# Passage from the projections to the branch products: four rows loaded over the freed activation, splits given out ahead, last merge gates in two buffers

## Chip, cores and metric

The kernel runs on one core of a Trainium2 chip. The metric is the time of one execution on the device, in microseconds (us). The profiler records one execution; the span is the time from its first instruction to its last.

## What is computed

Two layers over a sequence of 1024 rows with 1024 columns each. The change lies in the first one, `hybrid_layer`. Cut to what matters:

```python
u = layer_norm(x) * (1 + scale) + shift          # shift, scale, gate from silu(c) @ w_ada
proj = u @ w_in + b_in                           # ten projections, the last 3 x 1024 wide
y_a = pool branch of a_v * pool_scale * silu(a_g)
y_b = b_b * causal_dwconv(b_c * b_h) * silu(b_g)
y_c = silu(layer_norm(h_c)) * silu(c_g)          # h_c: causal_dwconv of 31 taps
g_m = sigmoid(merge)                             # three gates
m = g_m[0] * (y_a @ w_branch[0]) + g_m[1] * (y_b @ w_branch[1]) + g_m[2] * (y_c @ w_branch[2])
out = m @ w_out
return layer_norm(ALPHA * x + gate * out, ln_g, ln_b)
```

The second layer (attention, spatial gating and a gated MLP) follows and isn't touched.

## The kernel before

**Precision.** A float32 matrix product is made of three products of rounded parts: every operand is split into a high part (a cast on ACT) and a low part (a subtraction on DVE), `hilo` at L164. One product of 1024 by 1024 by 128 columns of weights, a slot, is 48 matmuls of 128 x 128 by 128 x 512: two halves of the columns, eight blocks k, three part products.

**Projections.** The transposed activation u lies on the chip as high part A0 and low part A1. Most projections run in pairs by a scheme with seven products of half size in place of eight (`run_two`, L395), whose operands are quarters of u and sums of quarters, held in B0 (high) and B1 (low). The order of the seven is 1, 6, 5, 2, 7, 3, 4; 1, 2 and 4 read quarters of u, the others read sums. The weights of a pair are split into parts a, b, c, d; five tiles on the right side of the memory hold them (`pair_tiles`, L1848), in this order from the start: a high, a low, c high, b low, c low; the high part of b lies elsewhere. In the trace, `A,w` and `B,w` are such products.

**Epilogues.** The results of a pair leave in `epi_store` (L832): one ACT operation (a sigmoid for the merge gates) into the tile e, and a store to DRAM from SP's queue. In the last part of the projections `n_e` is 1, so e is a single buffer: the second result waits until the store of the first has landed.

**The passage.** The last projections are those of a_v for group 0 and the last pair of merge gates (`add_merge`, i = 22). Then `pool_slot(0)` (L957) makes the pool products of that group: its `pre` empties the background queue, flushes the epilogue of the last pair, opens the pool ws for plain weights over the tiles of the pairs (two raw buffers wr from the start on, then two wh, then two wl, 1024 words each), starts the loads of the first branch weights (`dma_ahead`, L242), splits rows 0 to 3 of y_b, and splits the first weights (`split_ahead`, L251). Rows 0 to 3 of y_b have been loaded into raw and sums of the pool cw by `end` (L1020), during the last pair. `split_y` (L1035) writes the parts to new tiles over B0 and B1.

The results of the pool products, two rows of ya, leave through two buffers s (tag s, two of them, handed out in turn; the doubling sums of the pool use the same two before, an even number of times) and are stored from POOL's queue (L990).

`open_q` (L1048) closes the pools cw and ca and opens cq in their place. cw holds raw and sums, 2048 words each. ca begins behind it with pw (512 words), v (1040), and two s (1040 each); cn, ph, pl and others follow. cq is laid out in the order of first use: three g, one cb, four ld (tiles of 1024 words), mu_h, rs_h. So g and cb cover raw and sums. The second ld row that is handed out lies in the fourth place and covers part of the second s. A load into a new tile waits until the tiles below it are free. `open_q` loads the first gate g, rows 4 to 7 of y_b into ld, two more gates, splits the four rows, loads the statistics mu_h and rs_h and then c, and applies Silu to c on ACT.

**Branch products.** Slots d = 0 to 7 for branch 1 (y_b), then 0 (y_a), then 2 (y_c). For branch 1 and d = 0 the order is by k, so that the first half of the slot reads only rows 0 to 3. In `pre` a slot of branch 1 below d = 4 loads two rows of w_ada (`gate_dot`, L1095, into the ld tiles) and puts their dot products with silu(c) (DVE) in the background; the slot's result is multiplied by its gate on DVE behind them. Between d = 1 and d = 2 stands `stat_h` (products that sum mu_h and rs_h over the partitions, then moments, a reduction and a reciprocal root), between d = 2 and d = 3 `spread_h` (products `cst,wide` that spread its result).

Each engine and each DMA queue works in its own program order; waits are by semaphores between them.

Of the kernel before, what the change touches and what calls it, by code (L numbers as in the profile page):

```python
# [11 lines left out]
F = mybir.dt.float32  # L12
# [10 lines left out]
P = 128  # L23
# [83 lines left out]
class Kernel:  # L107
# [603 lines left out]
    def block1(self):  # L711
        nc, I = self.nc, self.I
        c0x, cwx = ExitStack(), ExitStack()
        T = {}
        d = lambda n, m=NK: [self.dram.tile([P, 1024], F, name="%s%d" % (n, i)) for i in range(m)]
        h_sp, ya_sp, yb_sp, ag_sp, cg_sp, mg_sp, m_sp = (
            d("h_sp"), d("ya_sp"), d("yb_sp"), d("ag_sp"), d("cg_sp"), d("mg_sp", 24), d("m_sp"))
# [33 lines left out]
        def e_tile():  # L751
            return self.c1.tile([P, 1024], F, tag="e", name="e", bufs=self.n_e)
# [78 lines left out]

        def epi_store(ct, func, sp, i):  # L832
            def one(ps, k):
                e = e_tile()
                self.act(e, ps, func, bias=self.bias_in(ct + k))
                nc.sync.dma_start(sp[i + k], e)
            return lambda x, y: [Task(0, lambda: one(x, 0)),
                                 Task(0, lambda: one(y, 1), 4 if self.n_e == 1 else 0)]

# [2 lines left out]
        def epi0():  # L842
# [13 lines left out]
                               name="start"))  # L856
# [39 lines left out]
        for what in "M G C5 B5 M M C6 G M B6 M C7 G M B7 M G M M".split():  # L896
# [4 lines left out]
            elif what[0] == "C":  # L901
                j = int(what[1])
# [54 lines left out]
        def pool_slot(g):  # L957
            s = {}

            def pre():  # L960
                while self.bgq:
                    self.bgq.popleft()()
                pairs.flush()
                if g == 0:
                    self.open_right("ws")
                    self.resume()
                    self.dma_ahead()
                    for j in range(4):
                        split_y(1, j)
                    self.split_ahead(1)  # L970

            def mm():
                wh, wl = T["pwr"]
                s["ps"] = [self.pair(), self.pair()]
                for c in range(2):
                    for h in range(2):
                        hs = slice(h * H, (h + 1) * H)
                        for k in range(2):
                            ph, pl = T["pool", 2 * g + k]
                            ks = slice((k * 2 + c) * P, (k * 2 + c + 1) * P)  # L980
                            self.mm3(s["ps"][c][:, hs], (wh[:, ks], wl[:, ks]), (ph[:, hs], pl[:, hs]),
                                     k == 0, k == 1)

            def one(c):
                if g:
                    e = e_tile()
                else:
                    e = self.c1.tile([P, 1040], F, tag="s", name="s", bufs=2)[:, 0:1024]
                self.act(e, s["ps"][c], AF.Identity, scale=self.par("pool_scale", 2 * g + c))
                (nc.sync if g else nc.gpsimd).dma_start(ya_sp[2 * g + c], e)  # L990

            def epi():
                pairs.todo = [Task(0, lambda c=c: one(c)) for c in range(2)]
                if g == 0:
                    pairs.flush()

            self.slots.append(Slot([], mm, epi, pre=pre, name="pool%d" % g))

        def open_a():
# [10 lines left out]
        for g, rest in ((3, "AA"), (2, "AM"), (1, "AM"), (0, "M")):  # L1010
            pair_u(A_V + 2 * g, A_V + 2 * g + 1, epi_av(g))
            for what in rest:
                if what == "M":
                    add_merge()
                else:
                    i = next(pool_gate)
# [14 lines left out]
        def open_y(n):  # L1031
            a, b = ("A0", "A1") if n == 0 else ("B0", "B1")
            T["Y", n] = (self.big(a, R), self.big(b, R))

        def split_y(n, j):  # L1035
            if ("Y", n) not in T:
                open_y(n)
            self.hilo(T["Y", n][0][:, j], T["Y", n][1][:, j], T["ld"].pop((n, j)))

        def load_y(n, j):  # L1040
            if j < 8 and (n, j) not in T["ld"]:
                t = T["ld"][n, j] = self.c1.tile([P, 1024], F, tag="ld", name="ld", bufs=4)
                nc.sync.dma_start(t, {0: ya_sp, 1: yb_sp, 2: h_sp}[n][j])
                if n != 1:
                    t = T["ld"]["g", n, j] = self.c1.tile([P, 1024], F, tag="ld", name="ld", bufs=4)
                    nc.sync.dma_start(t, (cg_sp if n else ag_sp)[j])

        def open_q():  # L1048
            self.ca.close()
            cwx.close()  # L1050
            self.ca = ExitStack()
            self.c1 = self.ca.enter_context(self.pool("cq", reuse_waits="tile"))
            T["g"], T["mi"] = {}, {}
            load_g(1, 0)
            T["g"][1, 1] = self.c1.tile([P, 1024], F, tag="g", name="g", bufs=3)
            T["g"][1, 2] = self.c1.tile([P, 1024], F, tag="g", name="g", bufs=3)
            T["cb"] = self.c1.tile([P, 1024], F, name="cb2")
            for j in range(4, 8):
                load_y(1, j)
            for j in (1, 2):  # L1060
                nc.sync.dma_start(T["g"][1, j], mg_sp[8 + j])
            for j in range(4, 8):
                split_y(1, j)
            self.mu_h = self.c1.tile([P, 1024], F, name="mu_h")
            self.rs_h = self.c1.tile([P, 1024], F, name="rs_h")
            nc.sync.dma_start(self.mu_h, st_sp[0])
            nc.sync.dma_start(self.rs_h, st_sp[1])
            nc.sync.dma_start(T["cb"], I["c"])
            self.act(T["cb"], T["cb"], AF.Silu)

        def load_g(n, d):
            if d < 8 and (n, d) not in T["g"]:
                T["g"][n, d] = self.c1.tile([P, 1024], F, tag="g", name="g", bufs=3)
                nc.sync.dma_start(T["g"][n, d], mg_sp[n * 8 + d])
                if n != 1:
                    T["mi"][n, d] = self.c1.tile([P, 1024], F, tag="mi", name="mi", bufs=2)
                    nc.sync.dma_start(T["mi"][n, d], m_sp[d])
# [33 lines left out]
        def branch(n, d, bg):  # L1111
# [37 lines left out]
            def epi():  # L1149
# [12 lines left out]
                else:  # L1162
# [3 lines left out]
                                   name="br%d.%d" % (n, d)))  # L1166

        self.slots.append(Slot(pre=open_q))
        held = len(self.slots)
        for n in (1, 0, 2):  # L1170
# [1058 lines left out]
```

## Time and profile before

| | us |
|---|---|
| three timed runs, median | 2711.1 |
| lowest and highest | 2710.7 and 2712.61 |
| the profiled execution | 2704.81 |
| its span | 2703.0 |

Microseconds in the rows count from the span's start. Engines: PE makes matrix products, PEld loads its weights, DVE and ACT work elementwise, POOL likewise, SP issues DMAs. "SPq" and "POOLq" are the DMA issues of these engines. L143 is the matrix product's helper line, L159 DVE's two-operand helper, L165 the cast in `hilo`, L156 the activation's helper, L247 the weight load, L1043 the load of a row into ld, L990 the store of ya. `B<-raw` and `B<-ld` are splits of y_b, `e<-pp` the merge gates, `s<-pp` the ya rows, `wh<-wr` and `wl<-wr` the parts of the weights. Brackets give the idle time of the engine just before and what ended it.

### The profile page before, as it was taken

The page shows a single profiled execution, that of the slowest core. Times are in us where ns is not written, and L with a number is a line of the kernel's source. Part 1 is how long each engine was busy: PE and PEld are TensorE (multiplying, and loading weights), DVE is VectorE, ACT ScalarE, POOL GpSimd, SP SyncE. Part 2 cuts the span into 40 slices and gives each one's busy share as a digit, 9 for nine tenths or more (in the row PEclk, how much of TensorE's full clock was granted, in tenths as well). Part 3 has the DMA queues.
Part 4 walks back from the last instruction along what each step waited for, and adds up shares of the span by engine and source line. Part 5 has one row for each costly group of instructions (what it writes and reads, how often), then busy time and mean ns, then how long its engine had stood idle before and what let it go on. Part 6 is the DMA issues. An engine that isn't in the chain of part 4 may idle for free.

```text
span 2703.0 us, 29526 instructions
## 1 busy us (share of the span) xinstructions
PE 2622.2 (97%) x11688; PEld 2143.6 (79%) x11688; DVE 1881.6 (70%) x2141; ACT 981.1 (36%) x1284; POOL 182.4 (7%) x178
## 2 busy tenths in 40 slices
PE   5999999999999997999999999999999999999998
PEld 3888887888788776877887788888888888887776
DVE  7789988899886664566564254546647788885576
ACT  5322233333343333222243255542323334343333
POOL 4000000000000000000032100000000000000220
PEclk9999999999999998999999999999999999999999
DMA  6111121222232225676342121112532222216964
GB/s 234 55 63 63 63 86 70 102 86 94 86 129 109 99 108 186 255 287 253 125 156 83 68 86 65 68 32 100 180 130 78 86 79 85 88 61 234 276 147 149
DMA packets 102380, 324.63 MB, mean 120 GB/s; under 512 B 11489, under 2 KB 12001, under 8 KB 102242
## 3 DMA queue, kind: packets, MB, share of 16 engines
q1 hardware_dynamic: 95474, 309.65, 31.9%
q0 software_dynamic: 6768, 13.11, 2.6%
q8 instruction: 91, 1.49, 0.2%
q14 instruction: 47, 0.39, 0.0%
HBM read 247.21 MB, written 75.50 MB: 119 GB/s over the span
## 4 chain that ended last, share of the span: by engine, by line
PE 75%; DVE 10%; DMA 7%; ACT 4%; issue 3%; SPq 1%; POOL 1%; DVEq 0%; ACTq 0%; POOLq 0%
PE pp L143 73%; DMA A<-g_sp 1%; DVE h L162 1%; DMA B<-x_sp 1%; DVE sums L159 1%; DVE ld L159 1%; DVE wl L159 1%; DVE A L159 1%; PE pm L143 1%; DVE g L159 1%; DVE B L159 1%; ACT e L156 1%; PE pp L146 1%; PE pm L146 1%; DMA mg_sp<-e 1%
## 5 line engine op out<-in xcount | busy, mean ns | idle before, releaser
L143 PE MATMUL pp<-A,wh 128*128 128x512 f32 x2432 | 769.7, 392 | 13.5 <-DVE A L159 9.0
L143 PEld LDWEIGHTS pp<-A,wh 128*128 128x128 f32 x2432 | 454.4, 188 | 115.1 <-DVE A L159 10.9
L143 PE MATMUL pp<-A,wl 128*128 128x512 f32 x1296 | 506.0, 390 | 2.8 <-DVE wl L159 2.8
L143 PE MATMUL pp<-B,A 128*128 128x512 f32 x1676 | 487.8, 390 | 1.2 <-DVE B L159 1.1
L143 PE MATMUL pp<-A,w 128*128 128x512 f32 x1664 | 443.4, 392 | 12.8 <-DVE pp L159 6.7
L143 PEld LDWEIGHTS pp<-A,w 128*128 128x128 f32 x1664 | 313.7, 189 | 83.3 <-DVE pp L159 10.3
L143 PE MATMUL pp<-B,w 128*128 128x512 f32 x1136 | 374.7, 389 | 0.0
L143 PEld LDWEIGHTS pp<-B,A 128*128 128x128 f32 x1676 | 313.9, 188 | 68.1 <-DVE B L159 2.3
L162 DVE SCALAR_TENSOR_TENSOR h<-p,par_t,h 128x1024 f32<-128x1024 f32 x240 | 312.8, 1303 | 4.7
L143 PEld LDWEIGHTS pp<-A,wl 128*128 128x128 f32 x1296 | 243.8, 188 | 55.4 <-DVE wl L159 4.5
L143 PE MATMUL pp<-B,wh 128*128 128x512 f32 x800 | 263.8, 395 | 15.6 <-ACT B L165 8.3
L159 DVE TENSOR_TENSOR wl<-wr,wh 128x1024 fp32r<-128x1024 f32 (+1 forms) x120 | 144.3, 1203 | 172.7 <-ACT wh L165 168.8
L143 PEld LDWEIGHTS pp<-B,w 128*128 128x128 f32 x1136 | 213.2, 188 | 44.3
L143 PEld LDWEIGHTS pp<-B,wh 128*128 128x128 f32 x800 | 151.3, 190 | 49.3 <-ACT B L165 9.2
L165 ACT CAST wh<-wr 128x1024 fp32r<-128x1024 f32 (+1 forms) x120 | 118.5, 989 | 188.3 <-PE pp L143 159.2
L162 DVE SCALAR_TENSOR_TENSOR z<-pp,par_t,z 128x1023 f32<-128x1023 f32 x88 | 112.6, 1280 | 48.0 <-ACT z L156 47.0
L143 PE MATMUL pp<-yh,xh 128*128 128x512 f32 x308 | 122.6, 398 | 5.9 <-ACT yh L165 5.9
L373 ACT CAST w<-raw 128x1024 fp32r<-128x1024 f32 x50 | 52.6, 1053 | 207.8 <-PE pp L143 141.0
L143 PE MATMUL pp<-yl,xh 128*128 128x512 f32 x308 | 123.1, 400 | 4.4 <-DVE yl L159 4.4
L143 PE MATMUL pp<-A,A 128*128 128x512 f32 x324 | 126.7, 391 | 0.1
L143 PE MATMUL pp<-B,wl 128*128 128x512 f32 x320 | 125.9, 393 | 0.0
L143 PE MATMUL pp<-yh,xl 128*128 128x512 f32 x308 | 121.1, 393 | 0.0
(278 smaller groups left out, 3187.4 us busy)
## 6 DMA issues: line engine op xcount, KB each, us to landing
raw<-in_w_in SPq DMA_DIRECT2D x66, 512.0 KB, 4.1
wr<-in_w_in SPq DMA_DIRECT2D x63, 512.0 KB, 3.5
raw<-in_w_up SPq DMA_DIRECT2D x34, 512.0 KB, 5.2
mg_sp<-e SPq DMA_DIRECT2D x24, 512.0 KB, 4.1
wr<-in_w_br SPq DMA_DIRECT2D x24, 512.0 KB, 5.9
g<-mg_sp SPq DMA_DIRECT2D x24, 512.0 KB, 5.4
A<-g_sp SPq DMA_DIRECT2D x44, 256.0 KB, 6.3
g_sp<-z SPq DMA_DIRECT2D x21, 512.0 KB, 3.0
```

The lines of the kernel that those rows point to most:

```text
L143: return self.nc.tensor.matmul(*a, **k)
L146: self.nc.tensor.transpose(*a)
L156: return self.nc.scalar.activation(out, in_, func, **kw)
L159: return self.nc.vector.tensor_tensor(out, a, b, op)
L162: self.nc.vector.scalar_tensor_tensor(out, a, s, b, op0, op1)
L165: self.nc.scalar.copy(hi, src)
L373: self.nc.scalar.copy(t.__dict__[which][0], src)
```

## The change

In `epi_store`, the last merge pair puts its second result into a buffer s, not into e, and both its results are stored from POOL's queue instead of SP's. In `pool_slot(0)`, the splits of rows 0 to 3 stand ahead of the flush of that pair's epilogue, not behind the start of the weight loads. Behind the weight loads, a new tile is opened over A0, and rows 4 to 7 of y_b are loaded into it from SP's queue. In `open_q` the loads of these four rows into ld are gone; their splits stay where they were and read the new tile.

```diff
@@ -831,9 +831,13 @@
 
         def epi_store(ct, func, sp, i):
             def one(ps, k):
-                e = e_tile()
+                last = sp is mg_sp and i == 22
+                if last and k:
+                    e = self.c1.tile([P, 1040], F, tag="s", name="s", bufs=2)[:, 0:1024]
+                else:
+                    e = e_tile()
                 self.act(e, ps, func, bias=self.bias_in(ct + k))
-                nc.sync.dma_start(sp[i + k], e)
+                (nc.gpsimd if last else nc.sync).dma_start(sp[i + k], e)
             return lambda x, y: [Task(0, lambda: one(x, 0)),
                                  Task(0, lambda: one(y, 1), 4 if self.n_e == 1 else 0)]
 
@@ -960,13 +964,18 @@
             def pre():
                 while self.bgq:
                     self.bgq.popleft()()
+                if g == 0:
+                    for j in range(4):
+                        split_y(1, j)
                 pairs.flush()
                 if g == 0:
                     self.open_right("ws")
                     self.resume()
                     self.dma_ahead()
-                    for j in range(4):
-                        split_y(1, j)
+                    t = self.big("A0", F)
+                    for j in range(4, 8):
+                        T["ld"][1, j] = t[:, j]
+                        nc.sync.dma_start(t[:, j], yb_sp[j])
                     self.split_ahead(1)
 
             def mm():
@@ -1055,8 +1064,6 @@
             T["g"][1, 1] = self.c1.tile([P, 1024], F, tag="g", name="g", bufs=3)
             T["g"][1, 2] = self.c1.tile([P, 1024], F, tag="g", name="g", bufs=3)
             T["cb"] = self.c1.tile([P, 1024], F, name="cb2")
-            for j in range(4, 8):
-                load_y(1, j)
             for j in (1, 2):
                 nc.sync.dma_start(T["g"][1, j], mg_sp[8 + j])
             for j in range(4, 8):
```

## Rows read from the trace of the kernel before

**Rows 1.** The page, section 1: busy us, share of the span, instructions.

```profile
PE 2622.2 (97%) x11688; PEld 2143.6 (79%) x11688; DVE 1881.6 (70%) x2141; ACT 981.1 (36%) x1284; POOL 182.4 (7%) x178
```

**Rows 2.** PE's timeline: start us, us, operation, out and in, count [idle before, releaser].

```profile
1035.42 2.88 PE L143 MATMUL pp<-B,A 128*128 128x512 f32 x12
...
1039.04 3.02 PE L143 MATMUL pp<-A,w 128*128 128x512 f32 x12 [0.74 <-DVE pp L159]
...
1047.15 0.39 PE L143 MATMUL pp<-ph,pwr 128*128 128x512 f32 x1
...
1053.62 1.22 PE L143 MATMUL pp<-B,wh 128*128 128x512 f32 x2 [6.08 <-ACT wh L165]
...
1068.67 0.79 PE L143 MATMUL pp<-B,wh 128*128 128x512 f32 x1 [7.42 <-ACT B L165]
...
1087.97 0.40 PE L143 MATMUL pp<-B,wl 128*128 128x512 f32 x1
...
1102.71 2.02 PE L143 MATMUL pp<-cst,wide 128*128 128x128 f32 x16
```

**Rows 3.** Windows: length, busy PE/PEld/DVE/ACT/POOL, granted PE clock, DMA share, GB/s.

```profile
1050.00:1055.00 5.00, 1.34 (x3) 0.62 (x3) 4.72 (x6) 3.80 (x5) 0.00 (x0) 0.54 0.59 217
```

**Rows 4.** ACT's timeline, columns as PE's.

```profile
1042.83 1.12 ACT L156 ACTIVATE e<-pp,par_t 128x1024 f32<-128x1024 f32 x1 [5.79 <-DVE pp L159]
...
1046.70 1.12 ACT L156 ACTIVATE e<-pp,par_t 128x1024 f32<-128x1024 f32 x1 [2.75 <-DMA mg_sp<-e]
...
1047.71 1.98 ACT L165 CAST B<-raw 128x1024 fp32r<-128x1024 f32 x2
...
1052.52 1.04 ACT L165 CAST wh<-wr 128x1024 fp32r<-128x1024 f32 x1 [0.94 <-DMA wr<-in_w_br]
...
1054.78 2.11 ACT L156 ACTIVATE s<-pp,par_t 128x1024 f32<-128x1024 f32 x2
...
1067.57 1.04 ACT L165 CAST B<-ld 128x1024 fp32r<-128x1024 f32 x1 [10.68 <-DMA ld<-yb_sp]
...
1079.91 1.28 ACT L156 ACT_TABLE_LOAD   x1 [5.42 <-DMA cb<-in_c]
```

**Rows 5.** Timeline of the DMA issues of SP's queue and of POOL.

```profile
1048.25 8.24 SPq L247 DMA_DIRECT2D wr<-in_w_br  x4
...
1056.22 0.80 POOL L990 DMA_DIRECT2D ya_sp<-s  x1 [25.47 <-ACT s L156]
...
1057.06 10.79 SPq L1043 DMA_DIRECT2D ld<-yb_sp  x4
...
1057.21 0.55 POOL L990 DMA_DIRECT2D ya_sp<-s  x1 [0.19 <-issue]
...
1070.12 0.83 SPq L1068 DMA_DIRECT2D cb<-in_c  x1
```

**Rows 6.** Waits of SP's queue, 1040 to 1120: us in total, times, longest.

```profile
SPq L1043 <- DMA ya_sp<-s: 9.1, 1, 9.1
```

**Rows 7.** DVE's timeline, columns as PE's.

```profile
1042.10 0.70 DVE L159 TENSOR_TENSOR pp<-pp,two 128x512 f32<-128x512 f32 x1 [2.31 <-PE pp L143]
...
1048.78 2.36 DVE L159 TENSOR_TENSOR B<-raw,B 128x1024 fp32r<-128x1024 f32 x2 [5.98 <-ACT B L165]
...
1053.60 2.54 DVE L159 TENSOR_TENSOR wl<-wr,wh 128x1024 fp32r<-128x1024 f32 x2 [0.19 <-ACT wh L165]
```

**Rows 8.** Tile wr, 1040 to 1115: its loads, from issue to landing.

```profile
DMA to landing us min/median/max: 3.4/4.2/7.5
```

**Rows 9.** Tile s, 1040 to 1115: its two stores, from issue to landing.

```profile
DMA to landing us min/median/max: 7.8/8.6/9.3
```

**Rows 10.** DMA issues of the whole run: count, KB each, median us to landing.

```profile
t<-in_w_dn POOLq DMA_DIRECT2D x11, 256.0 KB, 5.0
```

**Rows 11.** Timeline of POOL and DVE in the down-projection.

```profile
2488.05 1.90 POOL L1976 DMA_DIRECT2D B<-in_w_dn  x2 [13.03 <-ACT yh L165]
...
2489.24 0.69 DVE L159 TENSOR_TENSOR yl<-yr,yh 128x512 fp32r<-128x512 f32 x1
```

## Prediction

> **What bounds the kernel now.** I read the page first. PE is busy 97% of the span [rows 1], so a change of order can win only where PE stands still, or where it runs at its lower clock. I then read PE's timeline around the edited lines. The largest two holes lie in the passage that the diff touches: 6.08 us before the first branch product, and 7.42 us before the second half of that same product [rows 2]. The windows add that in 1050 to 1055 the granted clock is 0.54 of 2.4 GHz, which is the 1.2 GHz level for nearly the whole window [rows 3]. So the passage costs more than its holes.
>
> What ends each hole is told by the timelines of the other engines.
> - First hole. PE is done with the pool products at 1047.4 (last one 1047.15, next possible 0.23 later) [rows 2]. ACT passes the second merge gate only at 1046.70, held by the store of the first from the single buffer e [rows 4]. SP issues the branch weights behind the second gate's store, at 1048.25 [rows 5]. The weights land, ACT casts them at 1052.52, and PE starts at 1053.62.
> - Second hole. Rows 4 to 7 of y_b are loaded from 1057.06 on, and the second of these loads waits 9.1 us for a store of ya [rows 5, 6]; ACT casts row 4 at 1067.57 [rows 4].
> - Behind it stands the load of c, issued at 1070.12 after all of these and landed when ACT goes on at 1079.91 [rows 4, 5]. Silu(c), the adaLN dots and the statistics of h follow on ACT and DVE, up to the spread products, which start at 1102.71 [rows 2].
>
> **Scales.** Twelve products take 2.88 us with an end of 0.39 [rows 2], so one per (2.88 - 0.39) / 11 = 0.227 us, and one branch product (48) 10.9 us. The second branch product ends at 1087.97 + 0.23 = 1088.2, so the first ended at 1077.3. From 1088.2 to the spread at 1102.71 PE does the statistics and the third product: 14.5 us. From the landing of c to the spread it is 1102.71 - 1079.91 = 22.8 us, on ACT, DVE and SP; I take this stretch over as it is, since in it each step is issued by the one before.
>
> **Splits given out ahead.** Four high casts on ACT (1.98 per two [rows 4]) now stand before the merge gates. They write over the sums in B0/B1, last read by the product of 1035.42, which ends at 1038.3 [rows 2]. ACT is idle there until the gate at 1042.83 [rows 4], so the casts run 1038.3 to 1042.3 and cost nothing; without that cover they would cost 4.0. Their low parts stand on DVE behind the combination at 1042.10 [rows 7]: from 1042.8, four at 1.18 end at 1047.5, and the first weight's low part (1.2 [rows 7]) at 1048.7.
>
> **Merge gates.** The second gate takes a buffer s and no longer waits 2.75 us for a store [rows 4]: gates at 1042.83 and 1043.95, ending at 1045.0. The two stores go from SP to POOL, so SP has nothing before the weights. The first weight buffer lies over the pair's a, read last by the fourth of its seven products; the second over its c, free when the final product ends at 1042.0 (1039.04 + 3.02 [rows 2]). So SP issues the weights at 1042.1 at the latest, landing takes 4.2 (3.4 to 7.5 [rows 8]), and ACT casts them right behind the gates, 1045.0 to 1047.1. PE can start at 1047.4 and waits for the low part from 1047.9 to 1048.7: about 0.9 where it was 6.08. Its first 24 products then end at 1053.7, at full clock, since PE kept its clock after the hole of 0.74 at 1039.04, while both holes of over 6 us were followed by slow products [rows 2].
>
> **Rows 4 to 7 over A0.** The activation is read last by the product that ends at 1042.0; the four loads follow the weights on SP, 0.4 each, so 1042.5 to 1044. No later load is held, for SP had nothing else to do before. DMA is idle there. Row 4 lands near 1046.5, the last by 1054 (estimated, if the POOL stores take half of the engines from 1046 on). These loads wait no more for ya.
>
> **What the change adds.** Buffers s are two. The second gate now takes the one that is next, so the first ya row takes the other and the second ya row must wait until the gate's store has landed from POOL. Queued behind that ya row on ACT are the high casts of rows 4 to 7, and PE waits for those. POOL stores of 512 KB landed 7.8 and 9.3 after issue, some 0.3 after their ACT operation [rows 4, 5, 9]; the nearest lower row is 5.0 for 256 KB [rows 10]. I take 9.3, the second of a pair beside SP loads, which is the like case: issue 1045.3, landed 1054.6, ya 1.1 to 1055.7, high cast of row 4 1.05 to 1056.7, low cast to 1057.95, the remaining 23 products 5.2. The first branch product ends at 1063.2 against 1077.3: **PE's own gain 14.1**.
>
> The second added wait is on SP. The new pool's tiles start over raw and sums (4096 words: three g and c). With the ld rows gone from their place, mu_h and rs_h now come next: rs_h covers words 1024 to 2048 of the closed pool, and there, behind pw (512) and v (1040), begins the first s (at 1552). So the load of rs_h waits for the second ya store, and c and the adaLN rows stand behind it on SP. That is the 9.1 us wait of before [rows 6], moved. Ya issue 1056.0, landing 7.8 (the first of a pair in [rows 9]), 1063.8; rs_h issue 1063.9, c 1064.3, landing 4.6 (a load with one ahead, between 4.2 and the 7.5 of [rows 8]): 1068.9. The spread comes 22.8 later, 1091.7. PE is there at 1063.2 + 10.9 + 14.5 = 1088.6 and waits some 3. So c sets the end: **1102.7 - 1091.7 = 11.0 us**. Behind the spread the order and the bytes are those of before, so I carry the shift to the end.
>
> **Sum.** The profiled execution took 2704.81 (span 2703.0), the median is 2711.1, 6.3 more, spread over the whole run; the gain is taken off the median: 2711.1 - 11.0 = 2700.1. Bounds: with both POOL stores at 5.0, the second ends at 1050.3, the split is in time, the first product ends near 1059.2, PE reaches the spread at 1084.6 and c allows the same: gain 18.1, 2693.0. With 9.3 for both and 9.7 for c (issue 1070.12 to 1079.91 [rows 4, 5]): c at 1075.5, gain 4.4, 2706.7.
>
> **Rivals.**
> 1. *Quick stores* (5 to 6 us each): PE is the bound, 14.5 to 18.1 gained, about 2694. For it: DMA is idle before 1042. Against it: 7.8 and 9.3 [rows 9], the only POOL stores of this stretch. The Trainium skill ("DMA: Bandwidth & Descriptors", section on the anatomy of one DMA, SWDGE path) gives about 2.0 us plus bytes over 436 GB/s, an estimate of 3.2 for 512 KB; by it this rival would be the outcome, and the trace disagrees with 7.8 and 9.3 beside other traffic.
> 2. *POOL's issue is held while DVE works.* Then the gates' stores go out when DVE's low casts end, 1042.8 + 4.7 + 2.4 = 1049.9; landed 1059.5, ya store 1068.7, c 1073.8, gain 6.1: 2705.0. The Trainium skill ("SBUF — State Buffer", "SBUF: two separate sides") says that a DVE operation in a two-port mode keeps GpSimd from writing descriptors. Against it: POOL issued two loads in 1.90 us while DVE made such low casts, about its usual pace [rows 11].
> 3. *Late c*: the bound of 9.7 above, or a gain given back in later stages: 0 to 5 us, about 2707.
> 4. *Slower.* Two POOL stores in series now stand before c. With a for each, c lands at 1045.3 + a + 1.4 + a + 0.5 + 4.6 = 1051.8 + 2a. That meets 1079.9 of before at a = 14.1, and from there the change loses; at a = 18, because SP's 3 MB of weights, y rows and gates are served first, it loses 7.9: 2719.0. Against it: 9.3 is the largest landing of such a store [rows 9].
> 5. That A0 comes free later than I read: with the loads issued at 1047.4, after the pool products, row 4 would land near 1052, still ahead of ACT's turn at 1055.7. It changes nothing and goes with the forecast.
>
> **How the numbers follow.** Forecast 0.60, rival 1 0.17, rival 2 0.07, rival 3 0.10, rival 4 0.06. About 0.2% (5.4 us) is what a measurement of this kernel can tell from no change. Rival 2 lies at that edge, half to each side: faster 0.81, same 0.13, slower 0.06. The range 2692.5 to 2706.5 takes in the forecast, rivals 1 and 2 and the bounds, and leaves out most of 3 and all of 4.
>
> **What would show it.** PE's hole before the first branch product under 1.5; the hole before its second half 1 to 4, ended by ACT's cast of row 4, which follows the second ya row on ACT, which waits for the DMA of the gate's store. SP waiting at the load of rs_h for the ya store. ACT's Silu of c at 1066 to 1072, and a hole of some 3 us on PE before the spread. I am wrong if rs_h doesn't wait, if Silu stands after 1075, or if holes of several us appear behind the spread.

## The result, and the profile after

The changed kernel takes 2697.5 us (median of four runs, 2691.2 to 2700.5) against 2711.3: ratio 0.9945, 95% interval 0.9927 to 0.9963. That is faster by more than the 0.2% that can be told from no change, at 2.6 us under the forecast of 2700.1.

To compare traces, count from the start of the last pool product; it is the last product that PE makes alike in both programs. Two lengths serve for every kernel below. The **passage** goes from there to the start of the spread products. **Mark 4** is where DVE begins to multiply the fourth branch product's result by its gate; it takes in what a late spread or a low clock costs behind the passage. Before, the passage is 1102.71 - 1047.15 = 55.56 [rows 2], and mark 4 stands at 1115.67 - 1047.15 = 68.52. After, they are 1091.01 - 1045.22 = 45.79 and 1103.98 - 1045.22 = 58.76, both 9.8 less. Mark 4 in DVE's timeline, before and after:

```profile
1115.67 1.23 DVE L159 TENSOR_TENSOR g<-pp,g 128x1024 f32<-128x1024 f32 x1 [0.60 <-PE pp L143]
```

```profile
1103.98 1.22 DVE L159 TENSOR_TENSOR g<-pp,g 128x1024 f32<-128x1024 f32 x1 [0.67 <-PE pp L143]
```

The profiled spans differ by 2703.0 - 2689.4 = 13.6. Of that 1.9 lies ahead of the last pool product (1047.15 - 1045.22), 9.8 in the passage, and 1.9 behind it. The 1.9 ahead is there before the first instruction that stands elsewhere (the load of the first branch weight, issued at 1030.93 after): DVE makes a sum of the pool (`s<-v`) at 1031.83 before and at 1029.87 after. The passage is what the change did; the rest is taken up with the first experiment.

The page of the changed kernel, first its span, then section 1 (busy us, share of the span, instructions):

```profile
span 2689.4 us, 29519 instructions
...
PE 2616.5 (97%) x11688; PEld 2140.1 (80%) x11688; DVE 1880.0 (70%) x2141; ACT 980.4 (36%) x1284; POOL 183.2 (7%) x180
```

PE does the same 11688 products and shows the same 97% [rows 1]: the page can't tell where 10 us went. PE's timeline of the changed kernel can; it answers to [rows 2]:

```profile
1045.22 0.39 PE L143 MATMUL pp<-ph,pwr 128*128 128x512 f32 x1
...
1046.58 0.50 PE L143 MATMUL pp<-B,wl 128*128 128x512 f32 x1 [0.51 <-DVE wl L159]
...
1055.70 0.80 PE L143 MATMUL pp<-B,wh 128*128 128x512 f32 x1 [3.79 <-ACT B L165]
1056.96 0.80 PE L143 MATMUL pp<-B,wh 128*128 128x512 f32 x1 [0.46 <-DVE B L159]
...
1075.45 1.02 PE L143 MATMUL pp<-mu_h,cst 128*128 128x512 f32 x2
...
1091.01 2.02 PE L143 MATMUL pp<-cst,wide 128*128 128x128 f32 x16 [1.07 <-DVE wide L198]
```

The hole of 6.08 is now 0.51 (behind the first two products, where the weight's low part is awaited), that of 7.42 is 3.79, and a new one of 1.07 stands before the spread. What ends the second hole is seen on ACT, in its timeline (answers to [rows 4]):

```profile
1040.90 1.12 ACT L156 ACTIVATE e<-pp,par_t 128x1024 f32<-128x1024 f32 x1 [0.62 <-DVE pp L159]
1041.91 1.11 ACT L156 ACTIVATE s<-pp,par_t 128x1024 f32<-128x1024 f32 x1
1042.91 1.99 ACT L165 CAST wh<-wr 128x1024 fp32r<-128x1024 f32 x2
1044.80 1.12 ACT L156 ACTIVATE s<-pp,par_t 128x1024 f32<-128x1024 f32 x1
1053.60 1.11 ACT L156 ACTIVATE s<-pp,par_t 128x1024 f32<-128x1024 f32 x1 [7.68 <-DMA mg_sp<-s]
1054.61 3.88 ACT L165 CAST B<-A 128x1024 fp32r<-128x1024 f32 x4
1068.30 1.28 ACT L156 ACT_TABLE_LOAD   x1 [9.81 <-DMA cb<-in_c]
```

The two gates follow each other without a wait, and the weights are cast right behind them. The first ya row takes the free s, the second (1053.60) waits 7.68 for the store of the gate in the other s, and the four casts of the rows over A0 (`B<-A`) stand behind it. Those rows had been there for some 3 us: the last of their loads was issued by 1042.2, and the slowest took 9.3. The last line is the table for Silu, the moment at which c is there.

POOL's timeline and then SP's, with the waits of SP's queue (answers to [rows 5, 6]):

```profile
1042.35 0.80 POOL L840 DMA_DIRECT2D mg_sp<-e  x1 [13.57 <-ACT e L156]
1043.34 0.55 POOL L840 DMA_DIRECT2D mg_sp<-s  x1 [0.19 <-issue]
...
1055.00 0.53 POOL L999 DMA_DIRECT2D ya_sp<-s  x1 [8.26 <-ACT s L156]
```

```profile
1040.36 1.82 SPq L978 DMA_DIRECT2D A<-yb_sp  x4
...
1049.82 0.43 SPq L1073 DMA_DIRECT2D mu_h<-st_sp  x1
1061.97 0.32 SPq L1074 DMA_DIRECT2D rs_h<-st_sp  x1
1062.35 1.52 SPq L1075 DMA_DIRECT2D cb<-in_c  x1
```

```profile
SPq L1074 <- DMA ya_sp<-s: 11.6, 1, 11.6
```

SP issued everything up to mu_h by 1050.3 and then stood 11.6 us at the load of rs_h, for the store of the second ya row. The wait of 9.1 at the load of row 5 [rows 6] has moved there, as foretold, and c is behind it.

The DMA issues from 1040 to 1065 (KB each, us from issue to landing), and the windows of three stretches (columns as [rows 3]), both of the changed kernel:

```profile
mg_sp<-e POOLq DMA_DIRECT2D x1, 512.0 KB, 8.6
mg_sp<-s POOLq DMA_DIRECT2D x1, 512.0 KB, 10.2
```

```profile
1047.00:1051.00 4.00, 4.00 (x19) 3.27 (x18) 0.66 (x1) 0.00 (x0) 0.00 (x0) 1.00 1.01 384
1055.00:1061.00 6.00, 4.84 (x11) 3.46 (x12) 4.63 (x4) 3.48 (x4) 0.53 (x1) 0.50 1.03 423
1062.00:1068.00 6.00, 6.00 (x28) 4.91 (x27) 0.00 (x0) 0.00 (x0) 0.00 (x0) 1.00 0.77 253
```

The stores land late, and meanwhile all DMA engines are in use (share 1.01 in the first window); e5_no_a0 below shows what they take without the four loads. The second window is the one that the prediction didn't have: behind the hole of 3.79 the granted clock is 0.50 of 2.4 GHz, so 1.2 GHz, and 11 products pass in 6 us, of which PE is busy 4.84, where 28 pass in the third window.

### The profile page after: what moved, and what is told of

Its sections match the earlier page's. It is cut to its first block, busy times and chain, and to the rows that moved or that the text cites. A ratio compares the mean times of both kernels' runs of the same rounds, so it can differ in the third digit from the quotient of the medians.

```text
span 2689.4 us, 29519 instructions
## 1 busy us (share of the span) xinstructions
PE 2616.5 (97%) x11688; PEld 2140.1 (80%) x11688; DVE 1880.0 (70%) x2141; ACT 980.4 (36%) x1284; POOL 183.2 (7%) x180
## 4 chain that ended last, share of the span: by engine, by line
PE 73%; DVE 11%; DMA 7%; ACT 4%; issue 3%; SPq 1%; POOL 1%; ACTq 0%; DVEq 0%; POOLq 0%
PE pp L143 71%; DMA ld<-h_sp 2%; DVE h L162 1%; DVE g L159 1%; DVE A L159 1%; DVE sums L159 1%; DMA yr<-in_w_dn 1%; PE pm L143 1%; DVE B L159 1%; ACT e L156 1%; DVE wl L159 1%; DVE yl L159 1%; PE pp L146 1%; PE pm L146 1%; DMA ld<-ag_sp 1%
## 5 line engine op out<-in xcount | busy, mean ns | idle before, releaser
L143 PEld LDWEIGHTS pp<-A,wh 128*128 128x128 f32 x2432 | 454.4, 188 | 115.9 <-DVE A L159 10.9
```

What stands on the lines that cost most here:

```text
L143: return self.nc.tensor.matmul(*a, **k)
```

## Experiments

Each kernel was timed against the kernel before on the same chip, and all compute the whole result. The gain is 2710 times one less the ratio, in us, with its interval; the columns "earlier" and "mark 4 earlier" come from the profiled executions and say by how much the passage is shorter and mark 4 earlier than before.

| kernel | passage | earlier | mark 4 earlier | ratio | gain (interval) |
|---|---|---|---|---|---|
| after, first measurement | 45.79 | 9.8 | 9.8 | 0.9945 | 14.9 (10.0 to 19.8) |
| e0_after | 46.32 | 9.2 | 9.2 | 0.9956 | 11.9 (8.1 to 15.7) |
| e1_ya_v | 43.78 | 11.8 | 9.9 | 0.9957 | 11.7 (8.1 to 15.4) |
| e2_ld_first | 45.07 | 10.5 | 10.6 | 0.9960 | 10.8 (7.0 to 14.6) |
| e3_both | 44.43 | 11.1 | 9.1 | 0.9955 | 12.2 (8.4 to 16.0) |
| e5_no_a0 | 47.99 | 7.6 | 7.7 | 0.9967 | 8.9 (6.0 to 11.9) |
| e6_splits_back | 45.03 | 10.5 | 10.5 | 0.9959 | 11.1 (6.8 to 15.2) |
| e7_gates_back | 49.51 | 6.0 | 3.7 | 0.9980 | 5.4 (3.3 to 7.9) |
| e4_gates_sp | 46.97 | 8.6 | 7.0 | 0.9979 | 5.7 (3.3 to 8.4) |
| e10_dots_only | 45.49 | 10.1 | 10.2 | 0.9961 | 10.6 (6.8 to 14.1) |
| e8_late_dots | 37.18 | 18.4 | 18.5 | 0.9930 | 19.0 (16.0 to 22.2) |
| e9_late_dots_ld | 37.16 | 18.4 | 18.5 | 0.9936 | 17.3 (14.1 to 20.9) |

Read the columns "mark 4 earlier" and "gain" together: what mark 4 shows is what the whole time shows, within each interval (only the first measurement lies 0.2 outside). So the traces of the passage may be used to say what a part is worth. That some of the gain is given back later isn't seen, as far as intervals of 3 to 5 us either way can tell.

### The change again

No edit; the kernel after, timed a second time.

> The changed kernel itself, to place its gain. In the two profiled executions the passage, from the last projection product to the spread products, shrank by 9.7 us; another 1.97 us lie ahead of it and 1.9 behind it, where both programs are the same. Theory A (these 3.9 us are drift between executions): about 9.7 us faster than before, ratio 0.9964. Theory B (they belong to the change, by a mechanism not yet seen): about 13.6 us faster, ratio 0.9950.

Gain 11.9 where the first measurement had 14.9, and 9.2 in the passage. By the medians it is 2697.5 against 2707.4, so 9.9. The interval, 8.1 to 15.7, takes in both theories (9.7 and 13.6), so the times alone don't decide. The trace does: here the last pool product starts at 1047.83, 0.7 later than before, and from the spread to the end of the span it takes 0.2 less than before (1600.1 and 1600.3, against 1598.4 in the first profile). Neither of the two 1.9 us came back; they are differences between executions, as theory A has it.

### The second ya row in another buffer

```diff
                     e = e_tile()
+                elif c:
+                    e = self.c1.tile([P, 1040], F, tag="v", name="v")[:, 0:1024]
                 else:
```

> The second ya row goes to the buffer v, which is free, so that ACT no longer waits for the POOL store of the second merge gate. Both theories: the hole of 3.8 us before the second half of the first branch product goes, and with it the ten slow products behind it; that product ends 8.6 us earlier. Theory A (c sets the end next to PE): mu_h and rs_h now wait for this ya row's store, issued some 8 us earlier, so c lands about 5.5 us earlier and the spread products come 5 to 6 us earlier than in the changed kernel; PE idles some 4 us before them. Theory B (PE alone sets the end): 8 to 9 us earlier, with no such hole. Theory C (the POOL queue or DMA is the limit): under 2 us.

The second hole of PE is gone, as expected: the `mu_h,cst` products stand 22.85 behind the last pool product, against 30.23 after. The total didn't follow. From this kernel, PE's timeline, ACT's timeline, and two windows:

```profile
1092.34 3.75 PE L143 MATMUL pp<-cst,wide 128*128 128x128 f32 x16 [5.15 <-DVE wide L198]
```

```profile
1069.26 1.28 ACT L156 ACT_TABLE_LOAD   x1 [13.38 <-DMA cb<-in_c]
```

```profile
1055.00:1065.00 10.00, 10.00 (x46) 8.29 (x45) 1.23 (x1) 0.89 (x1) 0.00 (x0) 1.00 1.01 398
1092.00:1096.00 4.00, 3.66 (x17) 3.69 (x18) 4.00 (x7) 0.00 (x0) 0.00 (x0) 0.50 0.21 85
```

c was there 1069.26 - 1048.56 = 20.7 behind the last pool product, only 2.4 earlier than after (23.1). The store of the second ya row now goes out from v, over which mu_h lies, and SP waits at mu_h for it (9.4 us). It was issued 7.8 earlier than after, but it took 12.0 to land where it took 6.8, in traffic that fills the DMA engines (share 1.01). PE, 7.4 earlier, waits 5.15 for the spread, and then the granted clock is 0.50: 2.0 us gained at the spread are 0.2 at mark 4. The stall went from one place to the other.

### The first adaLN row's tile ahead of the statistics

```diff
             T["cb"] = self.c1.tile([P, 1024], F, name="cb2")
+            T["w0"] = self.c1.tile([P, 1024], F, tag="ld", name="adag", bufs=4)
...
-            w = self.c1.tile([P, 1024], F, tag="ld", name="adag", bufs=4)
+            w = self.c1.tile([P, 1024], F, tag="ld", name="adag", bufs=4) if d else T["w0"]
```

Now mu_h and rs_h lie further on, and no ya store holds c. Of the adaLN rows behind it only the second waits for a ya store, the first one, by 1.9 us.

> A tile ld is handed out ahead of mu_h and rs_h, so that these two lie where they lay before the change and wait for no ya store; the load of c is no longer held behind them. Theory A (two nearly equal ends): c lands 5 us or more earlier, the hole of 1.1 us before the spread products goes and nothing else, since PE is there 1.1 us later by its own path: 0.5 to 1.1 us faster than the changed kernel. Theory B (c alone sets the end, as the prediction had it, PE being there 3 us earlier): 3 us faster. Theory C: same.

c was issued 1056.13 - 1049.60 = 6.5 behind the last pool product, 10.6 earlier than after, but took 13.5 to land: it came at 1069.65 - 1049.60 = 20.05, 3.0 earlier than after and not the 5 of the expectation. The hole before the spread is gone. The spread is 0.7 earlier than after, little under the 1.07 that PE had waited; the total can't be told from that of after. With c early, PE itself is the bound.

### Both

The two edits above together.

> Both edits together: the second ya row in v, and a tile ld ahead of mu_h and rs_h. The first adaLN row now waits for the store of that ya row, c doesn't. Theory A: PE's own path sets the end, the spread comes 7 to 8.6 us earlier than in the changed kernel, more than the sum of the two single edits (6 to 7). Theory B (PE alone): 8 to 9, no more than the first edit alone. Theory C (POOL queue): under 2.

PE's timeline of this kernel, then the issue of c on SP, its landing on ACT, and a window:

```profile
1093.50 3.75 PE L143 MATMUL pp<-cst,wide 128*128 128x128 f32 x16 [4.97 <-DVE wide L198]
```

```profile
1055.52 0.33 SPq L1078 DMA_DIRECT2D cb<-in_c  x1
```

```profile
1070.60 1.28 ACT L156 ACT_TABLE_LOAD   x1 [14.02 <-DMA cb<-in_c]
```

```profile
1056.00:1070.00 14.00, 14.00 (x63) 11.60 (x62) 1.23 (x1) 0.58 (x1) 0.00 (x0) 1.00 1.03 416
```

The expectation is missed: a hole of 4.97 stands before the spread, and mark 4 is no earlier than after. The first adaLN dots waited on DVE for Silu of c (1072.98; their rows were there), and they stand ahead of the statistics of h. c itself was issued 6.45 behind the last pool product and no longer held by SP, but with the DMA engines full it took 15.0 to land and was there only at 21.53. The same shows in all five kernels with one of these two edits: c comes 20.0 to 21.5 behind the last pool product, whether it goes out at 6.1 (e9_late_dots_ld) or at 14.9 (e1_ya_v). What is in flight sets its landing; to issue it earlier isn't enough while the dots wait for it.

### The dots one slot later, with the second ya row in v

To the edit of e1_ya_v comes this. A slot's last number is how many background steps it takes in behind its products; with 0 the first slot leaves its two dots to the next one, and so on, and what is left is emptied ahead of d = 4:

```diff
                 if n == 1 and d == 4:
+                    while self.bgq:
+                        self.bgq.popleft()()
                     self.open_psum(3, 2)
...
-                branch(n, d, 2 if n == 1 else 1)
+                branch(n, d, (2 if d else 0) if n == 1 else 1)
```

> The second ya row in v (as in the run e1_ya_v), and the adaLN dots of each slot given out one slot later, so that the first branch result no longer waits on DVE for c and the first rows of w_ada; the work is the same. Theory A (c's chain took back what e1_ya_v gained): no hole over 1 us before the spread products, which come at 37 to 39 after the pool products instead of 46.3 and 43.8; 7 to 9 us faster than the changed kernel if nothing later is a bound, 0.9925 of before. Theory C (DMA in the branch stage is the bound): the spread comes at 38 too, but the start of the second branch's products stays at about 108 and the total gains under 2.

The same edit of the dots without v:

> The changed kernel with the adaLN dots given out one slot later, the second ya row left in s. Theory A (PE's holes and c's chain end almost together, so each hides the other): the hole of about 4.2 us before the second half and the slow products stay, the spread comes at 45 instead of 46.3 with no hole before it, 0 to 2 us faster than the changed kernel; with e1_ya_v at no gain either, the 9 us of e8_late_dots belong to both edits together. Theory B (the dots alone were the bound): spread at 37, 6 us or more faster.

And with the edit of e2_ld_first added to e8_late_dots:

> The kernel of e8_late_dots with a tile ld handed out ahead of mu_h and rs_h, so that these two no longer wait for the ya store; the first adaLN row does. Theory A (PE's own path is the bound in e8_late_dots): same as e8_late_dots within 1 us, spread at 37, no hole before it; the total says how far that kernel's 0.993 of before repeats. Theory B (mu_h and rs_h still bind): 2 us or more faster.

PE's timeline of e8_late_dots and a window of it; then PE's timeline of e10_dots_only:

```profile
1085.86 1.95 PE L143 MATMUL pp<-cst,wide 128*128 128x128 f32 x16
```

```profile
1080.00:1090.00 10.00, 10.00 (x54) 8.58 (x53) 8.14 (x26) 2.06 (x2) 1.68 (x1) 1.00 0.61 233
```

```profile
1063.02 0.80 PE L143 MATMUL pp<-B,wh 128*128 128x512 f32 x1 [4.54 <-ACT B L165]
...
1097.30 1.95 PE L143 MATMUL pp<-cst,wide 128*128 128x128 f32 x16
```

In e8_late_dots the spread stands at 1085.86 - 1048.68 = 37.18, with no hole before it and the clock at 1.00. That is PE's own work and no more: 0.23 + 0.51 + two products of 10.9 + 14.5 = 37.0 by the prediction's scales. The gain is 19.0, and its interval (16.0 to 22.2) lies beyond those of e1_ya_v and e10_dots_only, which have one half of the edit each and gain no more than the change alone. In e10_dots_only nothing holds the spread any more, but PE comes late to it by its own hole of 4.54. So the passage after has two ends of nearly the same length, PE's (second ya row, casts) and that of c and the dots, and each hides what is won at the other. In e8_late_dots c is no earlier than in e1_ya_v (20.6 and 20.7); what is won is that the statistics no longer stand behind its dots. e9_late_dots_ld gives the same again; with the dots out of the way the place of the tile is worth nothing. At 2691.0 us (median; 2691.8 for e9_late_dots_ld) these are the two fastest kernels here.

### Parts of the change undone, one at a time

Rows 4 to 7 loaded into ld again, not over A0:

```diff
-                    t = self.big("A0", F)
-                    for j in range(4, 8):
-                        T["ld"][1, j] = t[:, j]
-                        nc.sync.dma_start(t[:, j], yb_sp[j])
...
+            for j in range(4, 8):
+                load_y(1, j)
```

> Only the loads over A0 are undone: rows 4 to 7 of y_b go to ld tiles again, in the order of before. From the last pool product to the spread products the changed kernel took 46.3 us in its second profile, before 55.6. Theory A (the stores from s and what waits for them set the end): rows 5 to 7 wait for the two ya stores, the last until 17 after the pool products, c lands at about 29 instead of 23.4, the spread comes at about 52: 5 to 6 us slower than the changed kernel, 3 to 4 faster than before. Theory B (each part pays by itself a third): 3 us slower. If the loads over A0 carry all: as slow as before.

The DMA issues of this kernel, and PE's waits (us in total, times, longest):

```profile
mg_sp<-e POOLq DMA_DIRECT2D x1, 512.0 KB, 3.2
mg_sp<-s POOLq DMA_DIRECT2D x1, 512.0 KB, 3.6
```

```profile
PE pp L143 <- ACT B L165: 7.0, 1, 7.0
```

The hole of 7 us is back, as expected, but the passage is 47.99 and not 52: without the four loads on SP's queue the gates' stores landed in 3.2 and 3.6 us in place of 8.6 and 10.2, and so the ya rows, and the loads behind them, came earlier. The loads over A0 take away 3.2 us of the second hole and lengthen the stores by 5 to 7 us. What is left is worth 2.1 at mark 4 against the first profile of the change, 1.6 against e0_after; the total's 3.0 (11.9 and 8.9) lies within the intervals.

The splits of rows 0 to 3 behind the start of the weight loads again (the lines of the diff moved back):

> Only the splits of rows 0 to 3 go back, behind the last gates' epilogue and the start of the weight loads. PE's first hole grows from 0.9 to about 4, since the weights' parts come behind the four splits on DVE; the second hole shrinks by the same, since it ends by the POOL store of the second gate, which doesn't move. Theory A: the spread comes at 46 as in the changed kernel, within 1 us, total the same within 1 us. Theory B (each part pays by itself): 3 us slower.

PE's waits in this kernel:

```profile
PE pp L143 <- ACT wh L165: 2.2, 1, 2.2
PE pp L143 <- DVE wide L198: 2.1, 1, 2.1
PE pp L143 <- DVE wl L159: 1.0, 1, 1.0
```

Left late, the splits cost PE 3.2 in two holes of the first half, but after, PE stands 3.8 at the second half for the gate's store, and that hole is gone here: the time is lost earlier instead. Neither mark 4 (0.7 earlier than after) nor the total (0.8 less gain, within the intervals) shows a value of this part.

The gates in the single e again, stored from SP:

```diff
-                last = sp is mg_sp and i == 22
-                if last and k:
-                    e = self.c1.tile([P, 1040], F, tag="s", name="s", bufs=2)[:, 0:1024]
-                else:
-                    e = e_tile()
+                e = e_tile()
                 self.act(e, ps, func, bias=self.bias_in(ct + k))
-                (nc.gpsimd if last else nc.sync).dma_start(sp[i + k], e)
+                nc.sync.dma_start(sp[i + k], e)
```

> Only the merge gates go back to one buffer e and SP's queue. The first hole returns to about 6 us with slow products behind it, because the weights are issued behind the second gate's store; the second hole goes, because the second ya row finds a free buffer s. The second ya store is issued at about the same time (10 after the pool products). Theory A: spread at 46 to 48, total 0 to 2 us slower than the changed kernel. Theory B (each part pays by itself): 3 us or more slower. Theory C (the POOL stores only harm): 2 us or more faster.

PE's waits in this kernel, and a window:

```profile
PE pp L143 <- ACT wh L165: 6.5, 1, 6.5
PE pp L143 <- DVE wide L198: 4.5, 1, 4.5
```

```profile
1095.00:1101.00 6.00, 4.67 (x19) 4.51 (x20) 5.37 (x7) 0.88 (x1) 0.46 (x1) 0.50 0.38 149
```

The expectation is missed by 5 us: this part is worth 6.1 at mark 4 and 6.5 in the total, the most of the three. I had reckoned that the first hole comes back and the second goes. It did: 6.48 for 3.79. But the ya stores went out among the loads of weights, rows and gates. Here the first ya row takes the s that rs_h covers; its store was issued 9.4 behind the last pool product and landed at 17.5, so rs_h and c went out 0.7 later than after, and c took 8.7 to land for 5.9: it was there at 26.7 (23.1 after), PE waited 4.54 at the spread, and the clock fell behind it.

Only the queue undone, the buffer s kept (`(nc.gpsimd if last else nc.sync)` is `nc.sync`):

> The changed kernel with the two last gates stored from SP's queue again, the second gate still in s. The weights are issued behind these stores, 5.5 after where the first of them was issued in the changed kernel; rows 4 to 7 follow. Theory A: a first hole of 4 to 6 us with slow products, no second hole, since the second ya row finds its buffer free by 2; its store is issued at about 7 instead of 10, c lands 1 to 3 us earlier, spread at 43 to 46, total within 2 us of the changed kernel. Theory D (POOL's queue itself is the slow one): the gates' stores land 3 after issue on SP, the ya stores 7 to 10 on POOL with the same loads beside them. Theory E (sharing, not the queue, makes them slow): the gates' stores, issued ahead of the loads, land within 4, and ya as in the changed kernel.

PE's waits in this kernel, and its DMA issues:

```profile
PE pp L143 <- ACT wh L165: 4.1, 1, 4.1
PE pp L143 <- DVE wide L198: 3.1, 1, 3.1
```

```profile
mg_sp<-e SPq DMA_DIRECT2D x1, 512.0 KB, 2.7
mg_sp<-s SPq DMA_DIRECT2D x1, 512.0 KB, 3.3
ya_sp<-s POOLq DMA_DIRECT2D x2, 512.0 KB, 9.1
```

Missed too: slower than after by 4.8 (medians, 2702.3 and 2697.5) to 6.2 (gains), not within 2. The stores that went first in the traffic landed in 2.7 and 3.3, those of ya behind the loads in 9.1. The two differ in queue as well, so two more rows are needed: POOL's stores took 3.2 and 3.6 in e5_no_a0, and a store from SP's queue among loads was as slow as POOL's. It is that of the first branch result in e8_late_dots, issued at 1064.48 (DMA share 0.99 from 1064 to 1074):

```profile
m_sp<-g SPq DMA_DIRECT2D x1, 512.0 KB, 9.9
```

So what makes a store slow here is what is in flight beside it, not its queue. But on SP the gates stand ahead of the weights, which cost PE 4.1 before the first product, and both holes here were followed by low clock.

## Why the prediction was right, and where its terms were off

All times here count from the last pool product (1047.15 in the prediction, 1045.22 in the trace).

| step | predicted | measured |
|---|---|---|
| hole in the first branch product, for the weight's low part | 0.9 | 0.51 |
| its first half ends | 6.55 | 6.53 |
| the gate's store has landed, ya goes on | 7.45 | 8.38 |
| second half starts | 9.55 | 10.48 |
| SP issues the load of rs_h | 16.75 | 16.75 |
| first `mu_h,cst` product | 41.05 - 14.1 = 26.95 | 30.23 |
| c has landed | 21.75 | 23.08 |
| spread | 44.55 | 45.79 |

**Held.** The first hole, the second row's wait for the gate's store, and the wait of SP at rs_h are where and as large as foretold, to 1 us. That SP goes on at 16.75 in both columns is luck: the second ya store was issued 0.9 later (9.8 for 8.85) and landed 1.0 sooner (6.8 for 7.8). From c to the spread it is 22.7, where 22.8 was carried over. The total's gain at the passage is 9.8 for 11.0, and c's chain ended last, by 1.07.

**Mis-sized: PE's own gain, 14.1 against 41.05 - 30.23 = 10.8** (before, these products start at 1088.2 - 1047.15 = 41.05). The step that failed is that the remaining 23 products, and the one before them, run at full clock. I had seen that holes of 6 and 7 us were followed by slow products and one of 0.74 wasn't, and put the expected hole of 3 on the side of the latter, without a row for it. It was followed by 0.50 (the second window above). From the start of the second half to the end of the first product, which is 10.9 ahead of the `mu_h,cst` products, it took 30.23 - 10.9 - 10.48 = 8.85 in place of 6.5. With the start 0.9 later (the gate's store took 10.2 for 9.3) that is the whole of the 3.3.

**Mis-sized: c's landing.** 5.9 from issue to landing for 4.6, the whole of the 1.3 by which c was late. The 4.6 was put near the lower end of the 4.2 to 7.5 of [rows 8]; the measured 5.9 lies between them, at a DMA share of 0.77 (the third window).

Of the two errors only c's reached the sum, 1.2 at the spread. PE's 3.3 was hidden by the 3 that PE was to wait there, of which 1.07 is left; this is why the sum came out near. The prediction didn't see that the ends would be that close, and so that neither end alone is worth anything from here (e1_ya_v, e10_dots_only). That the time of the first measurement lies within 2.6 of the forecast is in part luck as well: it holds 4 to 5 us that aren't the passage's.

**The rivals.** Quick stores (rival 1) didn't happen here: 8.6 and 10.2. The price of 3.2 that the prediction took from the Trainium skill ("DMA: Bandwidth & Descriptors", anatomy of one DMA, SWDGE path) did show, but in e5_no_a0, where little but these two stores was in flight: 3.2 and 3.6. Rival 2, POOL's issue held by DVE, is refuted. DVE's timeline of the changed kernel:

```profile
1040.77 2.35 DVE L159 TENSOR_TENSOR B<-raw,B 128x1024 fp32r<-128x1024 f32 x2
1043.04 2.35 DVE L159 TENSOR_TENSOR B<-sums,B 128x1024 fp32r<-128x1024 f32 x2
```

In these 4.6 us POOL issued both gate stores in 0.80 and 0.55 (rows above), the same as the ya stores of before [rows 5]. In e5_no_a0 they went out beside the same subtractions and landed in 3.2 and 3.6, so these didn't hold the transfer either. The rule of the Trainium skill named there ("SBUF — State Buffer", "SBUF: two separate sides") speaks of DVE's two-port modes; that these subtractions hold POOL's issue, this trace does not show. Of rival 3 the first half (late c) came in part, 1.3 of its 6.6; the second (given back later) isn't seen, within the intervals. Rival 4 needed 14.1 per store; they took 10.2 and less. Rival 5, A0 free later, didn't arise: its loads were issued from 1040.36 on, and rows 4 to 7 were never waited for.

**Open.** Why executions differ by some us where the programs are the same, as in the first measurement. What a part is worth alone, put into the kernel before: only undoing was tried, and the values of the undone parts (6.1, 2.1, -0.7 at mark 4) need not add up to the 9.8, since each part's gain is cut by the end that comes next.

## What to carry to other kernels

Where a stage has two chains that end nearly together, a cure for either shows nothing; look up in the trace what comes second and how far behind it is, and move both (here 0 and 0 apart, 7 us together). When a pool is laid out anew, list for every queue the first load whose new place lies over a store still in flight: all that is issued behind it in order takes that wait, also what has nothing to do with the place. When a load comes late, see whether it was issued late or was long in flight: with the DMA engines full, c went out 8 us earlier and was there no earlier. And cost a hole of PE with the slow products that follow it.

## What the chip showed that was not expected

- A store of 512 KB from POOL's queue landed in 3.2 to 3.6 us with little beside it and in 8.6 to 10.2 beside four loads on SP's queue; from SP's queue it took 2.7 and 3.3 ahead of the loads and 9.9 among loads.
- The load of c, 512 KB as well, took 5.8 us when issued 14.9 behind the last pool product (e1_ya_v) and 15.0 when issued at 6.45 (e3_both), at a DMA share of 1.01 to 1.03 in the windows shown, and was there at 20.7 and 21.5.
- Holes of PE of 3.15 to 7.42 us were followed by a stretch at a granted clock of 0.50 or with such a part in it, in which products of 512 columns stand 0.43 us apart in place of 0.227. In e6_splits_back such a stretch followed two holes of 2.2 and 1.0 close together (granted clock 0.50 from 1051 to 1057). After holes of 0.5 to 2.1 that stood alone none was seen.
